# A second level of block products inside one product of an output projection

## The chip, the cores and the metric

The kernel runs on one core of a Trainium2 chip. The metric is the device time of one execution in microseconds (us). A core has five engines that run beside each other, each with its own queue of instructions: TensorE (PE in the profile; it multiplies, and loads its stationary operand as PEld), VectorE (DVE), ScalarE (ACT), GpSimd (POOL) and SyncE (SP), which here only starts transfers. Sixteen DMA engines carry the transfers. Matmul results land in PSUM, which has eight banks of 128 x 512 float32; everything else lies in SBUF or in the chip's main memory.

## The reference

One layer of a trunk with 512 tokens of width 2048, all in float32: a norm, an input projection, windowed attention with sinks, a gate, the output projection, then a gating stage with embeddings and a last norm.

```
hn = rmsnorm(x, norm_g)
q, k, v, gate = split(hn @ w_in)
out = windowed_attention(q, k, v, rel_bias, sinks)     # 512 x 2048
x = x + (out * silu(gate)) @ w_out                     # the output projection
emb = p @ ple_proj
g = sigmoid(rmsnorm(x, ple_norm) @ ple_gate)           # the gating stage
return rmsnorm(x + emb * g, final_g)
```

The change lies in the output projection, a product of a 512 x 2048 matrix (G, the gated attention) with the 2048 x 2048 matrix `w_out`.

## The kernel before, in words

**Precision.** TensorE takes its operands in a shorter format (`fp32r`). So each float32 operand is split into a high part and a low part, and `mm3` (lines 122 to 128) issues three matmuls for one: high x high (L126), high x low (L127), low x high (L128). For weights the high part is a cast on ScalarE (L679, tile `bhi`) and the low part a subtraction on VectorE (L680, tile `blo`). For the left operand it is L784 and L785 (tiles `fho` and `flo`).

**Seven products.** G is cut into four blocks, A11 and A12 (the first 256 tokens, low and high half of the features), A21 and A22 (the other tokens); `w_out` into B11, B12, B21, B22. The four blocks of G x `w_out` (c11 to c22) are built from seven block products instead of eight, each of 256 tokens x 1024 features x 1024 columns. They run in `ORDER_OUT`, 1, 7, 2, 6, 5, 3, 4. Product 2 is A12 x B21 and goes into c11 alone; product 1 (with a minus sign) goes into c11 too. Products 6, 5 and 3 go on adding into the PSUM banks of product 1 (the chain), so between them the banks are read out into x.

**Units and pieces.** A product is done by two calls of `unit`, one for each half `jj` of its columns. A unit takes four pieces of weights (m = 0 to 3). A piece is 128 x 1024: two blocks of 128 features with 512 columns. For a piece TensorE does 2 x 2 x 3 matmuls (two feature blocks, two blocks of 128 tokens, three of `mm3`). After the matmuls of a piece come, in the order in which the program is written: a share of `later` (additions of finished banks into x by `add_y`, L959 or L961, and the squares of finished rows, `squares`, L928, on ScalarE) and `todo` (one step of the next product's left operand, a load of x, or a turn).

**Weights.** `Pieces` hands out the pieces. `get(i)` issues the loads of later pieces and the splits of piece i + 2. There are three buffers each for raw weights, high and low parts; so the split of piece i + 2 waits until TensorE has read piece i - 1. Some products need sums of blocks of weights. These sums (`SUMS`) are made in main memory during attention, each by a copy (SP) and an adding transfer (POOL), in `sum_weights`. The pieces of products 6 and 4 share tiles (`grown`): those of 6 (seeds) are loaded by SP up to six pieces ahead, and once they are split an adding transfer from POOL turns them into those of 4.

**Turns.** In product 4, finished 128 x 128 blocks of x are transposed for the gating stage: `turn` does four transposes on TensorE (L942) and two scaled copies on ScalarE (L945). Product 4 makes 12 turns, two after a piece.

**Order on the engines.** TensorE and SP run in written order throughout (`manual_schedule`). VectorE, ScalarE and POOL have a written order in attention and in the gating stage from its second product on; in the output projection a planner orders them by its own forecast of what is ready. A queue runs in its order whichever way that was made.

Of the kernel before, what the change touches and what calls it, by code (L numbers as in the profile page):

```python
# [55 lines left out]
def trunk_kernel(ctx: ExitStack, tc: tile.TileContext, a: dict):  # L56
# [556 lines left out]

    def blk(t):
        return slice(t * P, (t + 1) * P)

    rooms = []

    ORDER_OUT, ORDER_PLE = (1, 7, 2, 6, 5, 3, 4), (2, 7, 1, 6, 5, 3, 4)

# [5 lines left out]
        return a[nm][2 * (c - 1) + jj, 4 * (r - 1) + m]  # L628

    SUMS = [("w_out", 7), ("w_out", 5), ("w_out", 6), ("ple_gate", 7), ("ple_gate", 5)]  # L630
    for nm, p in SUMS:
        for jj in range(2):
            for m in range(4):
                t = summed[nm, p, jj, m] = tc.dram_tile([P, WE], F32, name=f"{nm}_{p}_{jj}_{m}")
                first = {7: (1, 2), 5: (1, 1)}.get(p)
                copies.append((t, block(nm, *first, jj, m) if first else summed[nm, 7, jj, m]))
                adds.append((t, block(nm, *{7: (2, 2), 5: (1, 2), 6: (1, 1)}[p], jj, m)))
# [9 lines left out]
    class Pieces:  # L647
# [9 lines left out]
        def _prepare(self, i):  # L657
            kind, src, key = self.specs[i]
            if kind == "grow":
                t = self.grown[key]  # L660
                nc.gpsimd.dma_start(t, src, accum_op=ALU.add)
            else:
                if kind == "seed":
                    t = self.grown[key] = rooms[0].tile([P, WE], F32, tag="grown", name=f"grown{i}", bufs=8)
                else:

                    self.raws += 1
                    if rooms and i >= at_ple[ORDER_PLE[0], 0] and self.raws % 4 == 0:
# [24 lines left out]
        def ahead(self, i):  # L693

            last = len(self.specs) - 9
            for n in range(max(i, 0), min(i + 6, last) + 1):
                kind = self.specs[n][0]
                if n not in self.base and n >= self.done and kind != "grow" and (kind == "seed" or n <= i + (4 if i >= at_ple[ORDER_PLE[0], 0] else 3)):
                    self._prepare(n)
            while self.done <= min(i + 2, last):  # L700
                self._split(self.done)
                self.done += 1

        def get(self, i):
            self.ahead(i)

            key = self.specs[i][2]
            if key is not None:
                n = next((n for n in range(i + 1, len(self.specs)) if self.specs[n][2] == key), None)
                if n is not None:  # L710
                    self.due.append((i + 6, n))
            while self.due and self.due[0][0] <= i:
                self._prepare(self.due.pop(0)[1])
            return self.made.pop(i)
# [3 lines left out]
    def add_stage(nm, order):  # L718
        at = {}

        def add_embeds(p, jj):
            if nm == "ple_gate" and p in (1, 5, 3, 4):
                j = jj + 2 * (p in (5, 3))
                B.add("proj", a["ple_proj"].rearrange("(k p) d -> p k d", p=P)[:, :, j * 512 : (j + 1) * 512])

        for p in order:
            for jj in range(2):
                if nm == "ple_gate" and (p, jj) == (4, 0):
                    for v in range(2):
                        at["e", v] = len(B.specs)  # L730
                        add_embeds(p, v)
                at[p, jj] = len(B.specs)
                for m in range(4):
                    if (nm, p) in SUMS:
# [5 lines left out]
                    B.add(kind, src, (nm, jj, m) if p in growing else None)  # L740
                if p != 4:
                    add_embeds(p, jj)
        return at

    at_out = add_stage("w_out", ORDER_OUT)
    at_ple = add_stage("ple_gate", ORDER_PLE)

    class Forms:

# [5 lines left out]
        def steps(self, p):  # L755

            self.made[p] = []
            for h in range(2):
                a11, a21 = self.q[h][:, :, :256], self.q[h][:, :, 256:]
                a12, a22 = self.q[2 + h][:, :, :256], self.q[2 + h][:, :, 256:]  # L760
                if self.nm == "o":
                    src, sub = {
                        1: (a11, None), 7: (a11, (a21, a11)), 2: (a12, None), 6: (a11, (a22, a11)),
                        5: (a21, (a21, a22)), 3: (a12, (a12, a11)), 4: (a22, None),
                    }[p]
                else:
                    src, sub = {
                        2: (a12, None), 7: (a21, (a21, a11)), 1: (a11, None), 6: (a21, (a22, a21)),
                        5: (a11, (a11, a21)), 3: (a12, (a12, a21)), 4: (a22, None),
                    }[p]  # L770
# [129 lines left out]
        for _ in range(-(-len(later) // parts)):  # L900
            later.pop(0)()

    def unit(p, jj, at, forms, todo):

        ps = banks(p, jj, forms.nm)
        f = forms.made[p]
        first = p not in (6, 5, 3)
        for m in range(4):
            bh, bl = B.get(at[p, jj] + m)
            for kk in range(2):  # L910
                k = 2 * m + kk
                fh, fl = f[m]
                for tb in range(2):
                    mm3(ps[tb], fh[:, kk, blk(tb)], fl[:, kk, blk(tb)], bh[kk], bl[kk], first and k == 0, k == 7, not first)
            some_later(4 - m)
            todo()
        return ps


# [27 lines left out]
    ple_forms = Forms(hT, "g")  # L947
    ple_first = ple_forms.steps(2)

    def add_y(p, jj, tb, ps):  # L950
        c11, c12, c21, c22 = ((2 * v + jj, 2 * u + tb) for u in range(2) for v in range(2))
        whither = {
            1: [(c11, -1)], 2: [(c11, 1)], 7: [(c22, 1), (c21, -1)], 6: [(c21, -1)], 5: [(c22, 1)], 3: [(c12, 1)],
            4: [(c21, 1)],
        }[p]
        for (j, t), sign in whither:
            xt = x1[j][:, t, :]
            if sign > 0:
                nc.vector.tensor_add(xt, ps, xt)  # L959
            else:  # L960
                nc.vector.tensor_sub(xt, xt, ps)  # L961
            if p in (2, 5, 3, 4):
                squares(t, j)
# [5 lines left out]
    held = {}  # L969
    for n, p in enumerate(ORDER_OUT):  # L970
        nxt = out_forms.steps(ORDER_OUT[n + 1]) if n < 6 else iter(())
        for jj in range(2):
            later.extend(held.pop(waiting.get((p, jj)), ()))
            calls = iter(range(4))

            def todo():
                part = x_at.get((p, jj, next(calls)))
# [10 lines left out]
            ps = unit(p, jj, at_out, out_forms, todo)  # L988
# [12 lines left out]

# [83 lines left out]

    spare = late.tile([P, 2 * WE], F32R, name="spare")
# [12 lines left out]
    for n, p in enumerate(ORDER_PLE[:-1]):  # L1101
# [8 lines left out]
        for jj in range(2):  # L1110
# [16 lines left out]
            ps = unit(p, jj, at_ple, ple_forms, todo)  # L1127
            e = {}
            if p in (1, 5, 3):
                w = B.get(at_ple[p, jj] + 4)  # L1130
# [14 lines left out]
    def block(jj, tb, tag, e_tag, c=slice(0, 512)):  # L1145

        ps = bank(f"last{jj}_{tb}_{c.start}", tag)
        for k in range(8):
            fh, fl = f[k // 2]
            bh, bl = B.made[at_ple[4, jj] + k // 2]  # L1150
# [155 lines left out]
```

## Time and profile before

| | |
|---|---|
| median of 3 runs | 797.4 us (797.1 to 798.22) |
| the profiled execution | 797.26 us |
| its span, first to last instruction | 795.3 us |
| granted clock of TensorE, mean | 0.996 |
| output projection: matmuls into `o`, 672 | from 451.8 us to 609.3 us |

The profile's page gives for each engine its busy time and its share of the span; a table of groups (line, engine, operation, output <- inputs, shape, count | busy us, mean ns of one | idle time just before them and who ended it); the list of waits (who waited, for whom, in total, times, longest); the transfers; and, for any stretch, the instructions in order of time (start us, duration us, engine, line, operation). A line of stretches reads: from:to, length, then for each engine busy us and number of instructions, the granted clock, the DMA engines' busy share and GB/s. TensorE's matmuls overlap, so the duration of one is longer than the pitch at which they start.

### The profile page before, as it was taken

The page shows a single profiled execution, that of the slowest core. Times are in us where ns is not written, and L with a number is a line of the kernel's source. Part 1 is how long each engine was busy: PE and PEld are TensorE (multiplying, and loading weights), DVE is VectorE, ACT ScalarE, POOL GpSimd, SP SyncE. Part 2 cuts the span into 40 slices and gives each one's busy share as a digit, 9 for nine tenths or more (in the row PEclk, how much of TensorE's full clock was granted, in tenths as well). Part 3 has the DMA queues.
Part 4 walks back from the last instruction along what each step waited for, and adds up shares of the span by engine and source line. Part 5 has one row for each costly group of instructions (what it writes and reads, how often), then busy time and mean ns, then how long its engine had stood idle before and what let it go on. Part 6 is the DMA issues. An engine that isn't in the chain of part 4 may idle for free.

```text
span 795.3 us, 10980 instructions
## 1 busy us (share of the span) xinstructions
PE 785.0 (99%) x3758; PEld 657.6 (83%) x3758; DVE 587.3 (74%) x1026; ACT 500.6 (63%) x1057; POOL 116.2 (15%) x238
## 2 busy tenths in 40 slices
PE   9999999999999999999999999999999999999995
PEld 8888888888888888888888888888888888888885
DVE  4547697877878597777768898766646757988896
ACT  6643576666767576666757655555568656656765
POOL 0021213131212213121212100030000020200000
PEclk9999999999999999999999999999999999999998
DMA  9983489697869968787875479997603996787633
GB/s 348 271 218 110 117 259 242 172 254 183 226 168 255 206 198 230 192 238 158 247 170 146 119 264 328 352 261 239 205 30 132 373 211 194 159 227 218 180 106 106
DMA packets 42919, 165.28 MB, mean 208 GB/s; under 512 B 6048, under 2 KB 7072, under 8 KB 39024
## 3 DMA queue, kind: packets, MB, share of 16 engines
q1 hardware_dynamic: 35456, 129.67, 48.5%
q0 software_dynamic: 7408, 34.93, 23.9%
q8 instruction: 29, 0.48, 0.2%
q14 instruction: 26, 0.21, 0.1%
HBM read 157.70 MB, written 46.19 MB: 256 GB/s over the span
## 4 chain that ended last, share of the span: by engine, by line
PE 98%; DMA 0%; DVE 0%; ACT 0%; issue 0%; ACTq 0%; DVEq 0%
PE gps L126 7%; PE gps L128 7%; PE gps L127 7%; PE qps L126 7%; PE qps L128 7%; PE qps L127 7%; PE o L126 6%; PE o L128 6%; PE o L127 6%; PE g L126 5%; PE g L127 5%; PE g L128 5%; PE s L462 2%; PE o L557 2%; PE vps L279 2%; PE pt L515 2%
## 5 line engine op out<-in xcount | busy, mean ns | idle before, releaser
L680 DVE TENSOR_TENSOR blo<-braw,bhi 128x1024 fp32r<-128x1024 f32 x80 | 97.8, 1222 | 39.7 <-ACT bhi L679 39.5
L679 ACT CAST bhi<-braw 128x1024 fp32r<-128x1024 f32 x80 | 84.2, 1052 | 65.6 <-PE o L128 19.8
L126 PE MATMUL gps<-xh,whi 128*128 128x512 f32 x256 | 99.9, 390 | 0.1
L128 PE MATMUL gps<-xh,wlo 128*128 128x512 f32 x256 | 99.9, 390 | 0.0
L127 PE MATMUL gps<-xl,whi 128*128 128x512 f32 x256 | 99.8, 390 | 0.0
L126 PE MATMUL o<-bhi,fho 128*128 128x512 f32 x224 | 87.7, 392 | 0.0
L126 PE MATMUL qps<-xh,whi 128*128 128x512 f32 x224 | 87.7, 391 | 0.0
L128 PE MATMUL qps<-xh,wlo 128*128 128x512 f32 x224 | 87.4, 390 | 0.0
L127 PE MATMUL qps<-xl,whi 128*128 128x512 f32 x224 | 87.3, 390 | 0.0
L128 PE MATMUL o<-bhi,flo 128*128 128x512 f32 x224 | 87.2, 389 | 0.0
L127 PE MATMUL o<-blo,fho 128*128 128x512 f32 x224 | 87.2, 389 | 0.0
L110 DVE TENSOR_TENSOR wlo<-wraw,whi 128x1024 fp32r<-128x1024 f32 x60 | 73.8, 1231 | 2.7 <-ACT whi L109 2.4
L126 PE MATMUL g<-bhi,fhg 128*128 128x512 f32 x192 | 75.1, 391 | 0.0
L128 PE MATMUL g<-bhi,flg 128*128 128x512 f32 x192 | 74.8, 389 | 0.0
L127 PE MATMUL g<-blo,fhg 128*128 128x512 f32 x192 | 74.7, 389 | 0.0
L531 POOL TENSOR_SCALAR_AFFINE_SELECT own<-r 64x512 fp32r<-64x512 f32 (+1 forms) x48 | 32.5, 677 | 255.8 <-DVE r L521 255.8
L520 ACT CAST r<-pt 128x256 fp32r<-128x256 f32 x64 | 23.8, 371 | 71.5 <-PE pt L515 71.1
L521 DVE TENSOR_TENSOR r<-pt,r 128x256 fp32r<-128x256 f32 x64 | 27.1, 424 | 55.5 <-ACT r L520 54.8
L109 ACT CAST whi<-wraw 128x1024 fp32r<-128x1024 f32 x60 | 62.4, 1041 | 5.3 <-issue 3.9
L680 DVE TENSOR_TENSOR blo<-grown,bhi 128x1024 fp32r<-128x1024 f32 x32 | 39.1, 1224 | 23.5 <-ACT bhi L679 23.4
L128 PEld LDWEIGHTS gps<-xh,wlo 128*128 128x128 f32 x256 | 48.0, 188 | 10.1
L126 PEld LDWEIGHTS gps<-xh,whi 128*128 128x128 f32 x256 | 48.1, 188 | 9.4 <-PE vps L279 0.5
(207 smaller groups left out, 1736.5 us busy)
## 6 DMA issues: line engine op xcount, KB each, us to landing
wraw<-in_w_gate_in SPq DMA_DIRECT2D x32, 512.0 KB, 5.7
wraw<-in_w_q SPq DMA_DIRECT2D x28, 512.0 KB, 5.0
w_out<-in_w_out POOLq DMA_DIRECT2D x24, 512.0 KB, 7.1
braw<-in_w_out SPq DMA_DIRECT2D x24, 512.0 KB, 4.0
braw<-in_ple_gate SPq DMA_DIRECT2D x24, 512.0 KB, 4.2
xw<-in_first SPq DMA_DIRECT2D x14, 640.5 KB, 6.5
w_out<-in_w_out SPq DMA_DIRECT2D x16, 512.0 KB, 5.8
ple_gate<-in_ple_gate SPq DMA_DIRECT2D x16, 512.0 KB, 6.6
```

The source lines that it names most:

```text
L109: nc.scalar.copy(hi, raw)
L110: nc.vector.tensor_sub(lo, raw, hi.bitcast(F32))
L126: nc.tensor.matmul(ps, sh, mh, start=first, stop=False, skip_group_check=more)
L127: nc.tensor.matmul(ps, sh, ml, start=False, stop=False, skip_group_check=more)
L128: nc.tensor.matmul(ps, sl, mh, start=False, stop=last, skip_group_check=more)
L279: nc.tensor.matmul(v_ps[t], h[:, c], both[:, :, 256:512], start=f, stop=e, skip_group_check=True)
L462: nc.tensor.matmul(s_ps[:, u, : 2 * n], st, key[:, :, first : first + n], start=True, stop=True)
L520: nc.scalar.copy(rh, src)
L521: nc.vector.tensor_sub(rl, src, rh.bitcast(F32))
L531: nc.gpsimd.affine_select(out=flat(own), in_=flat(r).bitcast(F32), pattern=[[0, 8], [sign, HB]], compare_op=ALU.is_ge, fill=0.0, base=-HB ...
L679: nc.scalar.copy(hi, raw)
L680: nc.vector.tensor_sub(lo, raw, hi.bitcast(F32))
```

## The change

Product 2 leaves `ORDER_OUT`. In its place A12 x B21 is cut once more, into blocks of 128 tokens x 512 features x 512 columns, and made of seven small products (`small`) of two pieces each. The small products are put between the pieces of products 5, 3 and 4 by the table `SMALL`: 1 and 7 in product 5, 6 and 2 in product 3, 5, 4 and 3 in product 4. A small piece feeds 6 matmuls. The small products 1, 6, 5 and 3 chain in one bank of tag `t`; 4 takes the other bank of `t`, 7 and 2 banks of `o`. Four of the small products use sums of blocks of B21, made with the others during attention (8 more tiles, so 8 copies and 8 adding transfers more). The small left operands are made by `small_form` at the steps listed in `small_steps`. The additions into x go by `add_to_x`, which counts what a block of x still lacks and issues its square after the last.

Beside this: the left operand of product 3 is written over A11 instead of A12 (which the small products still read); a fourth buffer for raw weights is in use from product 6 on instead of from the gating stage on; the adding transfers of product 4's pieces are issued four `get`s later instead of six; the load of `final_g` moves from after product 6 to after product 3; the turns of product 4 come in another order and only through banks of tag `o`, two after each of the four pieces of its first half and after the last two of its second half. From product 7 to the end of product 3, VectorE and ScalarE run in written order.

```
-    ORDER_OUT, ORDER_PLE = (1, 7, 2, 6, 5, 3, 4), (2, 7, 1, 6, 5, 3, 4)
+    ORDER_OUT, ORDER_PLE = (1, 7, 6, 5, 3, 4), (2, 7, 1, 6, 5, 3, 4)
+
+    SMALL = {
+        (5, 0): {1: 1, 3: 1}, (5, 1): {1: 7, 3: 7}, (3, 0): {1: 6, 3: 6}, (3, 1): {1: 2, 3: 2},
+        (4, 0): {0: 5, 1: 5, 2: 4, 3: 4}, (4, 1): {0: 3, 1: 3},
+    }
...
-    for nm, p in SUMS:
+    def small_block(r, c, m):
+
+        return block("w_out", 2, 1, c - 1, 2 * (r - 1) + m)
+
+    for (nm, p), small in zip(SUMS, (7, 5, 6, 4, None)):
+        for m in range(2 if small else 0):
+            t = summed["small", small, m] = tc.dram_tile([P, WE], F32, name=f"small_{small}_{m}")
+            copies.append((t, {
+                7: small_block(1, 2, m), 5: small_block(1, 1, m), 6: summed.get(("small", 7, m)),
+                4: summed.get(("small", 6, m)),
+            }[small]))
+            adds.append((t, small_block(*{7: (2, 2), 5: (1, 2), 6: (1, 1), 4: (2, 1)}[small], m)))
...
-                    if rooms and i >= at_ple[ORDER_PLE[0], 0] and self.raws % 4 == 0:
+                    if rooms and i >= fourth_from and self.raws % 4 == 0:
...
-                    self.due.append((i + 6, n))
+                    self.due.append((i + (6 if i >= at_ple[ORDER_PLE[0], 0][0] else 4), n))
...
+    fourth_from = at_out[6, 0][0]
...
-                        5: (a21, (a21, a22)), 3: (a12, (a12, a11)), 4: (a22, None),
+                        5: (a21, (a21, a22)), 3: (a11, (a12, a11)), 4: (a22, None),
...
             some_later(4 - m)
             todo()
+            between(m)
...
+    def add_to_x(j, t, sign, ps):
+        xt = x1[j][:, t, :]
+        if sign > 0:
+            nc.vector.tensor_add(xt, ps, xt)
+        else:
+            nc.vector.tensor_sub(xt, xt, ps)
+        missing[j, t] -= 1
+        if not missing[j, t]:
+            squares(t, j)
...
+    def small_form(q):
...
+        if sub:
+            nc.vector.tensor_sub(src, *sub)
+            yield
+        if q == 1:
+            nc.scalar.mul(fh, src, -1.0)
...
+        else:
+            nc.scalar.copy(fh, src)
+            nc.vector.tensor_sub(fl, src, fh.bitcast(F32))
+        yield
...
+    small_steps = {
+        (6, 1, 2): 1, (5, 0, 0): 7, (5, 0, 2): 7, (5, 1, 0): 6, (5, 1, 2): 6, (3, 0, 2): 2, (3, 1, 0): 5, (3, 1, 2): 5,
+        (3, 1, 3): 4, (4, 0, 1): 3, (4, 0, 3): 3,
+    }
...
+    def small(q):
+
+        chained = q in (1, 6, 5, 3)
+        n = small_done[q] = small_done.get(q, -1) + 1
+        if n == 0:
+            if q == 1 or not chained:
+                small_ps[q] = bank(f"small{q}", "t" if chained or q == 4 else "o")
+            if chained:
+                small_ps[q] = small_ps[1]
+        bh, bl = B.get(at_out["small", q][n])
+        fh, fl = small_forms[q]
+        for kk in range(2):
+            k = 2 * n + kk
+            mm3(small_ps[q], fh[:, k], fl[:, k], bh[kk], bl[kk], k == 0 and q not in (6, 5, 3), k == 3, q in (6, 5, 3))
+        if n == 1:
+
+            to = {
+                1: [(0, 0, -1)], 2: [(0, 0, 1)], 7: [(1, 1, 1), (0, 1, -1)], 6: [(0, 1, -1)], 5: [(1, 1, 1)],
+                3: [(1, 0, 1)], 4: [(0, 1, 1)],
+            }[q]
+            later[:0] = [partial_of(add_to_x, *v, small_ps[q]) for v in to]
...
-    waiting = {(7, 0): (1, 0), (2, 0): (1, 1)}
+    waiting = {(7, 0): (1, 0), (6, 0): (1, 1)}
...
+        if n == 1:
+
+            middle.enter_context(
+                tc.manual_schedule(engines={getattr(mybir.EngineType, v) for v in ("PE", "SP", "DVE", "Activation")})
+            )
+        if p == 4:
+            middle.close()
...
+            def between(m):
+                q = small_steps.get((p, jj, m))
+                if q is not None:
+                    next(small_made.setdefault(q, small_form(q)))
+                q = SMALL.get((p, jj), {}).get(m)
+                if q is not None:
+                    small(q)
...
-                    for tag in "to":
-                        if turns:
-                            turn(*turns.pop(0), tag)
+
+                    for _ in range({0: 2, 1: 2, 2: 2, 3: 2, 6: 2, 7: 2}.get(4 * jj + step, 0)):
+                        turn(*turns.pop(0), "o")
...
-        if p == 6:
+        if p == 3:
             nc.sync.dma_start(fg, a["final_g"].partition_broadcast(P))
         if p == 3:
-            turns = [(kp, 0) for kp in range(8)] + [(kp, 1) for kp in range(4, 8)]
+            turns = [(kp, th) for kp0, th in ((4, 1), (4, 0), (0, 0)) for kp in range(kp0, kp0 + 4)]
```

More of the change, by code (lines that the diff above doesn't have):

```diff
@@ L697, in ahead @@
                 kind = self.specs[n][0]
-                if n not in self.base and n >= self.done and kind != "grow" and (kind == "seed" or n <= i + (4 if i >= at_ple[ORDER_PLE[0], 0] else 3)):
+                if n not in self.base and n >= self.done and kind != "grow" and (kind == "seed" or n <= i + (4 if i >= fourth_from else 3)):
                     self._prepare(n)
@@ L731, in add_stage @@
                         add_embeds(p, v)
-                at[p, jj] = len(B.specs)
+                at[p, jj] = []
                 for m in range(4):
+                    at[p, jj].append(len(B.specs))
                     if (nm, p) in SUMS:
@@ L740, in add_stage @@
                     B.add(kind, src, (nm, jj, m) if p in growing else None)
+                    q = SMALL.get((p, jj), {}).get(m) if nm == "w_out" else None
+                    if q is not None:
+                        v = at.setdefault(("small", q), [])
+                        src = summed.get(("small", q, len(v)))
+                        if src is None:
+                            src = small_block(*{1: (1, 1), 2: (2, 1), 3: (2, 2)}[q], len(v))
+                        v.append(len(B.specs))
+                        B.add("one", src)
                 if p != 4:
@@ L758, in steps @@
             for h in range(2):
-                a11, a21 = self.q[h][:, :, :256], self.q[h][:, :, 256:]
-                a12, a22 = self.q[2 + h][:, :, :256], self.q[2 + h][:, :, 256:]
+                a11, a21, a12, a22 = (
+                    self.q[v][:, :, c : c + 256] if v in self.q else None for v in (h, 2 + h) for c in (0, 256)
+                )
                 if self.nm == "o":
@@ L901, in some_later, with unit @@
             later.pop(0)()
-    def unit(p, jj, at, forms, todo):
+    def unit(p, jj, at, forms, todo, between=lambda m: None):
         ps = banks(p, jj, forms.nm)
@@ L908, in unit @@
         for m in range(4):
-            bh, bl = B.get(at[p, jj] + m)
+            bh, bl = B.get(at[p, jj][m])
             for kk in range(2):
@@ L948, in trunk_kernel @@
     ple_first = ple_forms.steps(2)
+    missing = {(j, t): {(0, 0): 1, (1, 0): 3, (0, 1): 1, (1, 1): 2}[t // 2, j // 2] for j in range(4) for t in range(NB)}
+    for part, n in {(0, 0): 2, (1, 0): 1, (0, 1): 3, (1, 1): 2}.items():
+        missing[part] += n
+    def add_to_x(j, t, sign, ps):
[7 more added lines that the diff above has]
+            squares(t, j)
@@ new lines, in trunk_kernel @@
+    halves = [gates[2 + h][:, :, :256].rearrange("p k (r t) -> p r k t", r=2) for h in range(2)]
+    sums_at = late.tile([P, 2 * WE], F32, tag="spare", name="small_sums")
+    sigma, tau = (sums_at[:, n * 512 : (n + 1) * 512].rearrange("p (k t) -> p k t", k=4) for n in range(2))
+    small_rooms, small_forms = [], {}
+    def small_form(q):
+        a11, a12, a21, a22 = halves[0][:, 0], halves[1][:, 0], halves[0][:, 1], halves[1][:, 1]
+        src, sub = {
+            1: (a11, None), 2: (a12, None), 4: (a22, None), 7: (sigma, (a21, a11)), 6: (sigma, (a22, sigma)),
+            3: (sigma, (a12, sigma)), 5: (tau, (a21, a22)),
+        }[q]
+        n = len(small_forms)
+        if n % 2 == 0:
+            small_rooms.append(late.tile([P, 2, 2, 512], F32, tag="partial", name=f"small_forms{n}", bufs=2))
+        fh, fl = (
+            small_rooms[-1][:, n % 2, v].bitcast(F32R).rearrange("p (k t) -> p k t", k=4) for v in range(2)
+        )
+        small_forms[q] = fh, fl
+        if sub:
[3 more added lines that the diff above has]
+            nc.scalar.mul(fh, src, -1.0)
+            nc.vector.scalar_tensor_tensor(
+                out=fl, in0=src, scalar=-1.0, in1=fh.bitcast(F32), op0=ALU.mult, op1=ALU.subtract
+            )
+        else:
+            nc.scalar.copy(fh, src)
+            nc.vector.tensor_sub(fl, src, fh.bitcast(F32))
+        yield
@@ new lines, in trunk_kernel @@
+    small_steps = {
+        (6, 1, 2): 1, (5, 0, 0): 7, (5, 0, 2): 7, (5, 1, 0): 6, (5, 1, 2): 6, (3, 0, 2): 2, (3, 1, 0): 5, (3, 1, 2): 5,
+        (3, 1, 3): 4, (4, 0, 1): 3, (4, 0, 3): 3,
+    }
+    small_made = {}
+    small_ps, small_done = {}, {}
+    def small(q):
[15 more added lines that the diff above has]
+                3: [(1, 0, 1)], 4: [(0, 1, 1)],
+            }[q]
+            later[:0] = [partial_of(add_to_x, *v, small_ps[q]) for v in to]
@@ L952, in add_y @@
         whither = {
-            1: [(c11, -1)], 2: [(c11, 1)], 7: [(c22, 1), (c21, -1)], 6: [(c21, -1)], 5: [(c22, 1)], 3: [(c12, 1)],
+            1: [(c11, -1)], 7: [(c22, 1), (c21, -1)], 6: [(c21, -1)], 5: [(c22, 1)], 3: [(c12, 1)],
             4: [(c21, 1)],
@@ L956, in add_y @@
         for (j, t), sign in whither:
[L957 to L963, printed above, removed]
+            add_to_x(j, t, sign, ps)
     turns = []
     x_at = {(1, 1, 1): 0, (7, 0, 0): 2, (7, 0, 3): 1, (7, 1, 1): 3}
-    waiting = {(7, 0): (1, 0), (2, 0): (1, 1)}
+    waiting = {(7, 0): (1, 0), (6, 0): (1, 1)}
     held = {}
+    middle = ExitStack()
     for n, p in enumerate(ORDER_OUT):
-        nxt = out_forms.steps(ORDER_OUT[n + 1]) if n < 6 else iter(())
+        if n == 1:
+            middle.enter_context(
+                tc.manual_schedule(engines={getattr(mybir.EngineType, v) for v in ("PE", "SP", "DVE", "Activation")})
+            )
+        if p == 4:
+            middle.close()
+        nxt = out_forms.steps(ORDER_OUT[n + 1]) if n < 5 else iter(())
         for jj in range(2):
@@ L974, in trunk_kernel @@
             calls = iter(range(4))
+            def between(m):
[3 more added lines that the diff above has]
+                q = SMALL.get((p, jj), {}).get(m)
+                if q is not None:
+                    small(q)
             def todo():
-                part = x_at.get((p, jj, next(calls)))
+                step = next(calls)
+                part = x_at.get((p, jj, step))
                 if part is not None:
@@ L981, in todo @@
                 if p == 4:
-                    for tag in "to":
-                        if turns:
-                            turn(*turns.pop(0), tag)
+                    for _ in range({0: 2, 1: 2, 2: 2, 3: 2, 6: 2, 7: 2}.get(4 * jj + step, 0)):
+                        turn(*turns.pop(0), "o")
                     if jj:
                         next(ple_first, None)
-            ps = unit(p, jj, at_out, out_forms, todo)
+            ps = unit(p, jj, at_out, out_forms, todo, between)
             posts = [partial_of(add_y, p, jj, tb, ps[tb]) for tb in range(2)]
@@ L1084, in trunk_kernel @@
     moved = []
-    spare = late.tile([P, 2 * WE], F32R, name="spare")
+    spare = late.tile([P, 2 * WE], F32R, tag="spare", name="spare")
     rooms4 = {}
@@ L1129, in trunk_kernel @@
             if p in (1, 5, 3):
-                w = B.get(at_ple[p, jj] + 4)
+                w = B.get(at_ple[p, jj][3] + 1)
                 for t in (0, 1) if p in (1, 3) else (2, 3):
@@ L1149, in block @@
             fh, fl = f[k // 2]
-            bh, bl = B.made[at_ple[4, jj] + k // 2]
+            bh, bl = B.made[at_ple[4, jj][k // 2]]
             mm3(ps[:, c], fh[:, k % 2, blk(tb)], fl[:, k % 2, blk(tb)], bh[k % 2][:, c], bl[k % 2][:, c], k == 0, k == 7)
```

## The prediction

> **What bounds the kernel now.** I read the profile's page first, then the list of waits, then single stretches. The page's first two parts and the waits of TensorE:
>
> ```profile
> span 795.3 us, 10980 instructions
> PE 785.0 (99%) x3758; PEld 657.6 (83%) x3758; DVE 587.3 (74%) x1026; ACT 500.6 (63%) x1057; POOL 116.2 (15%) x238
> L126 PE MATMUL o<-bhi,fho 128*128 128x512 f32 x224 | 87.7, 392 | 0.0
> ...
> PE warm_ps L141 <- PEq L1296: 0.9, 1, 0.9
> PE qps L265 <- ACT xh L224: 0.2, 1, 0.2
> ```
>
> TensorE is busy for 99% of the span, and its list of waits has two rows in all, both before the first real matmuls, 1.1 us together. From there to the last few microseconds it waits for nobody. So a matmul taken out of the middle is worth its pitch, and any wait put there costs its full length: nothing absorbs it. The pitch is not the 392 ns of the row, because matmuls overlap; it is the number started in a full stretch. The same stretches show how full the other engines and the DMA are (first the matmuls into `o` alone, then all):
>
> ```profile
> core 0: us, PE busy (x), PEclk, DMA share, GB/s
> 452.00:582.00 130.00, 130.00 (x575) 1.00 0.79 259
> ...
> core 0: us, PE busy (x) PEld busy (x) DVE busy (x) ACT busy (x) POOL busy (x), PEclk, DMA share, GB/s
> 100.00:450.00 350.00, 350.00 (x1730) 294.56 (x1730) 271.47 (x594) 235.23 (x645) 78.02 (x168) 1.00 0.78 205
> 452.00:496.00 44.00, 44.00 (x195) 36.43 (x195) 40.07 (x49) 23.97 (x31) 0.00 (x0) 1.00 0.78 274
> 496.00:541.00 45.00, 45.00 (x200) 37.26 (x200) 32.83 (x38) 24.41 (x33) 6.89 (x8) 1.00 0.98 293
> 541.00:582.00 41.00, 41.00 (x183) 33.96 (x182) 25.27 (x26) 21.58 (x31) 0.00 (x0) 1.00 0.61 206
> 582.00:610.00 28.00, 28.00 (x149) 23.71 (x148) 15.62 (x19) 22.41 (x45) 0.00 (x0) 1.00 0.11 38
> ```
>
> 575 matmuls in 130.00 us is 226 ns each. A piece of weights feeds 12 of them, 2.71 us; a product (8 pieces) takes 21.7 us.
>
> **Part 1: fewer matmuls.** Product 2 is 96 matmuls. The seven small ones are 7 x 2 pieces x 6 = 84. So 12 x 226 ns = **-2.71 us**. The 128x128 stationary and the 512 columns stay, so the pitch stays. Number and grouping of the transposes stay (12 turns in six pairs). [...]
>
> **Part 2: more side work.** Product 2's 8 pieces become 14, so six more splits; 4 more additions to x (8 instead of 4); form copies 7 instead of 4, and four small subtractions. Durations from the groups and the order of time before:
>
> ```profile
> L680 DVE TENSOR_TENSOR blo<-braw,bhi 128x1024 fp32r<-128x1024 f32 x40 | 48.9, 1223 | 20.0 <-ACT bhi L679 19.9
> L679 ACT CAST bhi<-braw 128x1024 fp32r<-128x1024 f32 x40 | 42.0, 1051 | 31.8 <-PE o L128 19.8 <-DMA braw<-w_out 7.6 <-DVE blo L680 2.1
> L785 DVE TENSOR_TENSOR flo<-gate,fho 128x512 fp32r<-128x512 f32 x24 | 16.5, 687 | 5.7 <-ACT fho L784 5.7
> L784 ACT CAST fho<-gate 128x512 fp32r<-128x512 f32 x23 | 14.3, 624 | 19.9 <-PE o L127 19.8
> L959 DVE TENSOR_TENSOR x1s<-o,x1s 128x512 f32<-128x512 f32 x20 | 13.1, 684 | 1.5 <-PE o L128 1.5
> ...
> 549.66 1.28 DVE L959 TENSOR_TENSOR x1s<-o,x1s 128x512 f32<-128x512 f32 x2
> 550.00 1.05 ACT L679 CAST bhi<-braw 128x1024 fp32r<-128x1024 f32 x1 [1.52 <-PE o L128]
> 550.96 0.62 ACT L928 ACTIVATE junk<-x1s 128x512 f32<-128x512 f32 x1
> 551.09 1.23 DVE L680 TENSOR_TENSOR blo<-braw,bhi 128x1024 fp32r<-128x1024 f32 x1
> 551.58 0.61 ACT L928 ACTIVATE junk<-x1s 128x512 f32<-128x512 f32 x1
> 552.46 0.62 ACT L784 CAST fho<-gate 128x512 fp32r<-128x512 f32 x1 [0.17 <-PE o L127]
> 552.99 1.04 ACT L679 CAST bhi<-braw 128x1024 fp32r<-128x1024 f32 x1
> ```
>
> VectorE gets 6 x 1.22 + 4 x 0.68 + 3 x 0.69 + 4 x 0.68 = 14.8 us more, on the 113.8 us that the four stretches from 452 to 610 add up to; ScalarE 6 x 1.05 + 3 x 0.62 = 8.2 us on 92.4. In some 155 us both still fit, at 83% and 65%. By total work this costs nothing. What can cost is order.
>
> **Part 3: less cover per piece, and a written order.** A piece is split two pieces ahead: its high part (ScalarE, L679) may start when TensorE leaves the buffer three pieces back, then VectorE makes the low part. With pieces of 2.71 us that is 5.42 us of cover. A small piece is 6 matmuls, 1.36 us; wherever one lies in the pair, cover is 4.07 us. The chain itself takes 0.2 us (release) + 1.08 (high, to the start of low) + 1.22 = 2.5 us, so 2.9 us of margin become 1.55.
>
> In the stretch before, the planner orders VectorE and ScalarE by what is ready. The change writes their order for products 7, 6, 5 and 3: split, addition to x, its square, forms, next split. What a written order costs is seen in the gating stage, which has one already:
>
> ```profile
> 677.90 0.68 DVE L1025 TENSOR_TENSOR s<-e,s 128x512 f32<-128x512 f32 x1
> 678.62 0.69 DVE L1029 TENSOR_TENSOR x1s<-x1s,s 128x512 f32<-128x512 f32 x1
> 679.34 0.63 ACT L1032 ACTIVATE s<-x1s 128x512 f32<-128x512 f32 x1 [1.29 <-DVE x1s L1029]
> 680.55 1.22 DVE L680 TENSOR_TENSOR blo<-grown,bhi 128x1024 fp32r<-128x1024 f32 x1
> 680.67 0.63 ACT L1032 ACTIVATE s<-x1s 128x512 f32<-128x512 f32 x1 [0.60 <-DVE x1s L1029]
> 681.30 2.20 ACT L679 CAST bhi<-grown 128x1024 fp32r<-128x1024 f32 x2
> 682.20 0.39 PE L126 MATMUL g<-bhi,fhg 128*128 128x512 f32 x1
> ```
>
> ScalarE stands 1.29 and 0.60 us at the squares until VectorE has added, and the split behind them starts late. The low part begun at 680.55 ends at 681.77, and its piece begins at 682.20: of 2.9 us of margin 0.4 are left. With 1.55 us such a meeting is a stall. [...]
>
> One place worked out, the last three pieces of product 5 and the first of product 3, from the start of (5, second half, m=1) as zero. TensorE starts: m=1 at 0, small 7 at 2.71, m=2 at 4.07, m=3 at 6.78, small 7 again at 9.49, product 3 at 10.85, its low part one matmul later, 11.1. ScalarE's written order: high of m=2 at 0.2; VectorE its low at 1.3, then the addition at 2.4 (1.14 us after the low's start), done at 3.1; square at 3.15; form copy 3.8; high of m=3 4.3, high of the small piece 5.3. VectorE: lows at 5.4 and 6.5, second addition 7.7, done 8.35. Square 8.4, the small form's copy 9.0, and only then the high of product 3's first piece, 9.55, though its buffer has been free since 7.0; low 10.65 to 11.87. Needed at 11.1: 0.8 us late, and 1.0 with the 0.2 that VectorE carries in. Stepping all of 7, 6, 5 and 3 through the written order in this way gives stalls at four places: 0.4 us where (6, second half) waits for the last addition of product 1, 1.0 us here, 1.5 us at (3, second half, m=0 and 1), 1.4 us at (3, second half, m=2) and the first piece of product 4. Together **+4.3 us**. Ends: 0, if the meetings fall as well as in the planner's order, where TensorE has no wait; 5.9, if ScalarE needs 0.88 us after each square (551.58 to 552.46) instead of 0.62.
>
> **Part 4: product 4.** Here the planner orders again, but six small pieces and all turns in the two `o` banks meet. ScalarE has 24 hT copies as before, and 14 pieces where there were 8. Ends: 0, as in the planner's product 4 before (no wait of TensorE), and 6.5 us, which stepping it in written order would give. The nearest row is the planner's own, so I take **+0.5 us**.
>
> **Part 5: transfers.** Four sums of two pieces add 8 copies and 8 accumulations to 40 and 40 while attention runs; six more loads; a fourth buffer two stages earlier; final_g moves from after product 6 to after product 3.
>
> ```profile
> braw<-w_out SPq DMA_DIRECT2D x16, 512.0 KB, 5.0
> x1s<-in_x SPq DMA_DIRECT2D x4, 1024.0 KB, 6.8
> grown<-w_out SPq DMA_DIRECT2D x8, 512.0 KB, 8.5
> grown<-in_w_out POOLq DMA_DIRECT2D x8, 512.0 KB, 10.5
> fg<-in_final_g SPq DMA_DIRECT2D x1, 1024.0 KB, 17.4
> ```
>
> Attention's DMA share of 0.78 rises by at most a fifth, to 0.94; the copies and accumulations are queued behind nothing that TensorE wants soon, since an attention weight is loaded two pieces, over 10 us, ahead. On POOL's queue eight more issues lie between masks. The seeds of product 6 now load beside x, in a stretch at 0.78, and the growing transfers follow at once beside the first pieces of product 5; a seed is asked for up to six pieces (16 us) ahead and lands in 8.5 us, a plain piece three or four ahead and in 5.0. final_g leaves the full stretch (0.98) for the empty one (0.11); TensorE waited for it nowhere, so that gains nothing. I take 0 for all of it; bounds -0.2 and +2 us, the latter being a wait of ScalarE for `braw<-w_out` that reaches TensorE where its group above has 7.6 us of them hidden.
>
> **Sum.** The profiled execution took 797.26 us (span 795.3 and 1.96 around it). 797.26 - 2.71 + 4.3 + 0.5 = **799.3 us**. The median of 797.4 is 0.14 above that execution, well inside what can be told apart: 0.2%, 1.6 us.
>
> **Rivals.**
> 1. *The queues keep up* (the other side). No handover is late; TensorE's list of waits stays empty and only part 1 remains: 797.26 - 2.71 = 794.6. It decides wherever the addition and its square are done within the 1.55 us of margin. For it: by total work both engines have room. Against: the 0.4 us left in the gating stage with longer pieces.
> 2. *Product 4 clogs.* The planner lines ScalarE up for readiness, and the four copies of two turns stand ahead of highs whose cover is now one small and one full piece; half to all of 6.5 us: 799.3 + 3 to 6 = 802 to 805. For it: ScalarE is busy 22.41 of 28 us there already.
> 3. *Part of the price:* only one or two of the four places stall, 1.1 to 4 us together, and the change is not measurable: 796 to 798.9.
>
> **How the numbers follow.** Forecast (798 to 801.5) 0.46, of which 0.06 lies under 799.0; rival 1 0.28; rival 2 0.12; rival 3 0.14. Faster than 795.8: 0.28. Between 795.8 and 799.0: 0.14 + 0.06 = 0.20. Slower: 0.40 + 0.12 = 0.52. The likeliest one's own range is 798 to 801.5; 8 in 10 need rival 1's end and the lower half of rival 2: 794.4 to 803.
>
> **What would show it.** Right: matmuls into `o` and the small banks 660 instead of 672; in TensorE's list of waits rows of some 1 us each, released by VectorE's low parts (L680's line), at about 547, 563 and 577 us; ScalarE waiting for VectorE at the squares there. Part 4 right: no such rows, or short ones, in product 4. Part 5 wrong: releases by transfers. The prediction is wrong if TensorE's busy time falls by 2.7 us and its idle time doesn't grow.

## The result and the profile after

The changed kernel takes 800.89 us (median of 6 runs, 800.65 to 802.06) against 797.49 us before (6 runs). The ratio is 1.0045, with a 95% interval of 1.0032 to 1.0058: it is slower by 3.4 us. The forecast was 799.3 us, slower. Of all the executions reported below one is far off, 2055.76 us in experiment 5, and it is not in the ratio there.

The profiled execution of the changed kernel is a long one of the six, 802.06 us. Its page and TensorE's list of waits (engine, line, waited for: us in total, times, longest):

```profile
span 800.4 us, 11030 instructions
PE 785.9 (98%) x3746; PEld 655.2 (82%) x3746; DVE 599.9 (75%) x1043; ACT 506.7 (63%) x1066; POOL 123.5 (15%) x246
...
PE o L127 <- DVE blo L699: 4.7, 5, 1.6
PE warm_ps L141 <- PEq L1415: 0.9, 1, 0.9
```

The 12 matmuls are gone (3746 instructions instead of 3758), and a row has come that was not there: TensorE waits for low parts of weights (L699 is the old L680). The row's 4.7 us count only from the modelled end of the matmul before, so they understate what is lost. The number of matmuls that start in a stretch tells it better:

```profile
core 0: us, PE busy (x) PEld busy (x) DVE busy (x) ACT busy (x) POOL busy (x), PEclk, DMA share, GB/s
496.00:541.00 45.00, 44.42 (x194) 36.00 (x193) 38.42 (x46) 23.27 (x29) 6.92 (x8) 1.00 0.97 280
541.00:582.00 41.00, 36.88 (x155) 28.21 (x154) 33.16 (x39) 25.80 (x40) 0.00 (x0) 1.00 0.63 212
582.00:615.00 33.00, 33.00 (x172) 27.85 (x171) 23.66 (x26) 26.84 (x50) 0.00 (x0) 1.00 0.34 112
100.00:450.00 350.00, 350.00 (x1731) 294.54 (x1730) 271.26 (x596) 235.64 (x645) 84.46 (x176) 1.00 0.85 229
```

From 541 to 582 us 155 matmuls start where 183 did before: 28 x 226 ns = 6.3 us. From 496 to 541 six fewer start, 1.4 us. From 582 us on, in product 4, TensorE is full again, and attention has as many matmuls as before (1731 and 1730) although its DMA share went from 0.78 to 0.85. So the loss sits in products 6, 5 and 3 and at the first piece of 4. The 7.7 us lost and the 2.7 us saved leave 5.0 us; the two profiled executions stand 4.8 us apart. That is more than the 3.4 us between the medians, since the profiled execution of the changed kernel lies 1.2 us above its median: by the medians the stalls cost 3.4 + 2.7 = 6.1 us.

The place that the prediction worked out, in the order of time (start us, duration us, engine, line, operation; in brackets the idle time before, and who ended it):

```profile
543.00 1.22 DVE L699 TENSOR_TENSOR blo<-braw,bhi 128x1024 fp32r<-128x1024 f32 x1
544.13 0.68 DVE L989 TENSOR_TENSOR x1s<-o,x1s 128x512 f32<-128x512 f32 x1
544.85 0.63 ACT L959 ACTIVATE junk<-x1s 128x512 f32<-128x512 f32 x1 [2.08 <-DVE x1s L989]
545.48 0.60 ACT L1024 CAST small_forms<-small_sums 128x512 fp32r<-128x512 f32 x1
545.79 0.39 PE L126 MATMUL small<-bhi,small_forms 128*128 128x512 f32 x1
545.99 2.94 ACT L698 CAST bhi<-braw 128x1024 fp32r<-128x1024 f32 x3
547.15 0.44 PE L126 MATMUL o<-bhi,fho 128*128 128x512 f32 x1
547.46 2.35 DVE L699 TENSOR_TENSOR blo<-braw,bhi 128x1024 fp32r<-128x1024 f32 x2
548.73 0.50 PE L127 MATMUL o<-blo,fho 128*128 128x512 f32 x1 [1.14 <-DVE blo L699]
549.06 0.39 PE L128 MATMUL o<-bhi,flo 128*128 128x512 f32 x1
```

ScalarE stands idle for 2.08 us at the square of a row until VectorE has added to it. Then it copies a small form, and only at 545.99 does it begin the high part of product 3's first piece. VectorE's low part follows at 547.46 and is done at 548.68. TensorE had begun that piece at 547.15 with the high part; its second matmul comes at 548.73, 1.58 us after the first where 0.23 us is usual. The third comes 0.33 us later, not 0.23: this stall costs another 0.1 us after it.

### The profile page after: what moved, and what is told of

Read it like the earlier page. It is cut to its first block, busy times and chain, and to the rows that moved or that the text cites. A ratio compares the mean times of both kernels' runs of the same rounds, so it can differ in the third digit from the quotient of the medians.

```text
span 800.4 us, 11030 instructions
## 1 busy us (share of the span) xinstructions
PE 785.9 (98%) x3746; PEld 655.2 (82%) x3746; DVE 599.9 (75%) x1043; ACT 506.7 (63%) x1066; POOL 123.5 (15%) x246
## 4 chain that ended last, share of the span: by engine, by line
PE 95%; DVE 2%; DMA 1%; ACT 1%; issue 1%; ACTq 0%; DVEq 0%
PE gps L126 7%; PE gps L128 7%; PE gps L127 7%; PE qps L126 7%; PE qps L128 7%; PE qps L127 7%; PE g L126 5%; PE g L127 5%; PE g L128 5%; PE o L127 5%; PE o L128 5%; PE o L126 5%; PE s L462 2%; PE o L557 2%; PE vps L279 2%; PE pt L515 2%
## 5 line engine op out<-in xcount | busy, mean ns | idle before, releaser
L699 DVE TENSOR_TENSOR blo<-braw,bhi 128x1024 fp32r<-128x1024 f32 x86 | 104.6, 1222 | 45.9 <-ACT bhi L698 45.7
L698 ACT CAST bhi<-braw 128x1024 fp32r<-128x1024 f32 x86 | 89.9, 1052 | 70.9 <-PE g L128 19.1
L127 PE MATMUL o<-blo,fho 128*128 128x512 f32 x192 | 75.6, 394 | 4.7 <-DVE blo L699 4.7
L126 PE MATMUL o<-bhi,fho 128*128 128x512 f32 x192 | 75.4, 393 | 0.0
L128 PE MATMUL o<-bhi,flo 128*128 128x512 f32 x192 | 74.8, 390 | 0.0
L495 ACT ACTIVATE t<-t,sm 128x129 f32<-128x129 f32 x128 | 50.6, 397 | 8.0 <-DVE sm L491 6.4
```

What stands on the lines that cost most here:

```text
L126: nc.tensor.matmul(ps, sh, mh, start=first, stop=False, skip_group_check=more)
L127: nc.tensor.matmul(ps, sh, ml, start=False, stop=False, skip_group_check=more)
L128: nc.tensor.matmul(ps, sl, mh, start=False, stop=last, skip_group_check=more)
L495: nc.scalar.activation(su, su, AF.Exp, bias=sm[:, u : u + 1], accum_out=sm[:, 2 + u : 3 + u])
L698: nc.scalar.copy(hi, raw)
L699: nc.vector.tensor_sub(lo, raw, hi.bitcast(F32))
```

## The experiments

The theory: in written order, ScalarE's queue holds the square of a finished row in front of the next split; the square waits for VectorE, and with the shorter cover of a small piece the split is then late. Rival A: the shorter cover is late under any order. Rival B: transfers land late, since more of them share the time. Each experiment ran with the kernel before on the same chip; ratios are to that.

**1. The planner's order again.** In the change, the block that writes the order is taken out:

```
-            middle.enter_context(
-                tc.manual_schedule(engines={getattr(mybir.EngineType, v) for v in ("PE", "SP", "DVE", "Activation")})
-            )
+            pass
```

> The change, but VectorE and ScalarE are ordered by the planner again in products 7, 6, 5 and 3. Theory (the written order puts a square, which waits for VectorE, in front of the next split): the waits of TensorE for low parts go, 794.8 us (797.5 - 2.7) to 795.6. Rival A (the shorter cover of small pieces is late under any order): about 800.9, as the change. Rival B (transfers land late): 800 to 801, with waits of the splits for loads as before them.

Measured: 796.48 us, ratio 0.9988 (0.9979 to 0.9997). Rival A falls: the same small pieces with the same cover, in another order, are 4.4 us faster. But the theory's range is missed by 0.9 us, and only 0.9 of the 2.7 us that the matmuls save are seen. TensorE's waits, in an execution of 797.39 us:

```profile
PE o L127 <- DVE blo L699: 2.3, 2, 1.5
PE warm_ps L141 <- PEq L1413: 0.9, 1, 0.9
PE o L126 <- ACT bhi L698: 0.3, 1, 0.3
```

Two stalls stay, at about 494 and 533 us. Before both, ScalarE is idle until a load lands, 0.66 and 2.70 us. At the first, VectorE then takes three steps for left operands (from 491.52 to 493.4) before the low part, which starts 2.1 us after the high part:

```profile
491.24 1.06 ACT L698 CAST bhi<-braw 128x1024 fp32r<-128x1024 f32 x1 [0.66 <-DMA braw<-w_out]
493.32 1.21 DVE L699 TENSOR_TENSOR blo<-braw,bhi 128x1024 fp32r<-128x1024 f32 x1
...
531.93 2.06 ACT L698 CAST bhi<-braw 128x1024 fp32r<-128x1024 f32 x2 [2.70 <-DMA braw<-w_out]
533.01 1.22 DVE L699 TENSOR_TENSOR blo<-braw,bhi 128x1024 fp32r<-128x1024 f32 x1 [2.53 <-ACT bhi L698]
```

**2. The written order without the small pieces.** The kernel before, with the same block around products 7 to 3:

```
+        if n == 1:
+            middle.enter_context(
+                tc.manual_schedule(engines={getattr(mybir.EngineType, v) for v in ("PE", "SP", "DVE", "Activation")})
+            )
+        if p == 4:
+            middle.close()
```

> The kernel before, with VectorE and ScalarE in written order from product 7 to product 3 and nothing else changed. Theory (written order costs only together with small pieces): margins of 2.9 us shrink but stay above zero, 797.3 to 798.0. If the written order cost the same with any pieces it would be 797.5 + 4 to 6 = 801.5 to 803.5. Rival A expects no change, 797.5.

Measured: 798.41 us, ratio 1.0009 (1.0000 to 1.0018): 1.0 us between the medians, nothing to 1.4 us by the interval; the median lies 0.4 us above the theory's range. The two waits that count, of ScalarE from 496 to 582 us and of TensorE in the whole span (of an execution of 797.69 us, one of the shortest of the eleven):

```profile
ACT junk L928 <- DVE x1s L959: 21.0, 10, 2.8
...
PE o L127 <- DVE blo L680: 0.4, 1, 0.4
```

ScalarE stands at its squares even longer here (21.0 us, ten times) than in the changed kernel (14.4 us, six times, in the same stretch), and yet a single short wait reaches TensorE. So neither the order alone nor the small pieces alone cost the 3.4 us: the two together do. The reading is that the order uses up margin, and that the small pieces have taken most of it away; that it is their shorter cover, and not what else came with them (more additions, forms and loads), is worked out in the prediction and not tested by itself.

**3. The square behind the next split.** In the change, still in written order, a finished row's square is put on a list, and the list is emptied right after the next `get` of a unit:

```
     def squares(t, j):
+        owed.append((t, j))
+
+    def square(t, j):
...
             bh, bl = B.get(at[p, jj][m])
+            owed_squares()
```

> The change, still in written order; only each square of a finished row is issued behind the next piece's split instead of in front of it. Theory: ScalarE no longer stands at a square while a split is due; stepping the queues gives 0.4 us of stall instead of 4.3, so 795.2, and up to 796.2 if the late load at about 530 us still costs its 0.7. Rival A: 800.9. Rival B: 800 to 801.

Measured: 795.30 us, ratio 0.9972 (0.9961 to 0.9983). It beats both kernels. No low part appears in TensorE's list of waits (by the starts of its matmuls two short stalls stay, 0.4 us each at 507 and 531 us), and around the same place as above ScalarE splits when TensorE releases the buffer and does the square afterwards:

```profile
PE warm_ps L141 <- PEq L1425: 0.8, 1, 0.8
PE o L126 <- DVE x1s L1001: 0.2, 1, 0.2
...
537.50 1.06 ACT L698 CAST bhi<-braw 128x1024 fp32r<-128x1024 f32 x1 [1.11 <-PE o L128]
538.14 0.68 DVE L999 TENSOR_TENSOR x1s<-o,x1s 128x512 f32<-128x512 f32 x1
538.86 1.06 ACT L698 CAST bhi<-braw 128x1024 fp32r<-128x1024 f32 x1 [0.30 <-PE small L128]
539.81 0.63 ACT L969 ACTIVATE junk<-x1s 128x512 f32<-128x512 f32 x1
540.44 0.61 ACT L1034 CAST small_forms<-small_sums 128x512 fp32r<-128x512 f32 x1
541.62 1.06 ACT L698 CAST bhi<-braw 128x1024 fp32r<-128x1024 f32 x1 [0.57 <-ACT small_forms L1034]
```

The addition that a square needs is done by 538.8, a split before ScalarE comes to it at 539.81: the same work, moved behind one instruction, waits for nobody.

**4. Plain loads into the growing pieces.**

```
-                nc.gpsimd.dma_start(t, src, accum_op=ALU.add)
+                nc.gpsimd.dma_start(t, src)
```

> The change, with the transfers from POOL into the growing pieces as plain loads instead of accumulating ones (the sums of weights of the last product of both stages are left out, so its result is another). Rival B: the 8 accumulating transfers crowd out the loads, so most of the stall goes, 796 to 797. Theory: only the stall where a split waited for a load (about 532 us, 0.7 us) goes, 799.8 to 800.4. Rival A: 800.9.

Measured: 799.98 us, ratio 1.0031 (1.0020 to 1.0043), 0.9 us less than the change between the medians; the two intervals overlap. Transfers from 490 to 535 us, first in the change, then here (tile, queue, count, size, median us to landing; and of POOL's queue, q0, packets, MB, share of the 16 engines' time):

```profile
braw<-w_out SPq DMA_DIRECT2D x8, 512.0 KB, 8.8
grown<-in_w_out POOLq DMA_DIRECT2D x8, 512.0 KB, 14.5
q0 software_dynamic: 1152, 4.19, 46.8%
```

```profile
braw<-w_out SPq DMA_DIRECT2D x8, 512.0 KB, 4.2
grown<-in_w_out POOLq DMA_DIRECT2D x8, 512.0 KB, 6.6
q0 software_dynamic: 1152, 4.19, 24.2%
```

The same bytes landed in less than half the time when they didn't accumulate (6.6 us instead of 14.5), and the eight loads beside them too (4.2 instead of 8.8). The stalls at about 532 and 543 us go. Those after 546 us stay, and the list of waits still has 3.5 us for low parts. So rival B is right about a part, and only that. The stall at 543 us is not the loads' alone: it goes in experiment 3 too, where the transfers accumulate as before. In the change ScalarE had stood at a square before that piece's split:

```profile
539.64 0.63 ACT L959 ACTIVATE junk<-x1s 128x512 f32<-128x512 f32 x1 [2.99 <-DVE x1s L989]
540.78 1.05 ACT L698 CAST bhi<-braw 128x1024 fp32r<-128x1024 f32 x1
```

After the late load at 531 us VectorE came late to the addition that this square needs: it begins it 3.2 us ahead of the piece's first matmul (538.92 and 542.15), and 4.2 us ahead with plain loads (536.62 and 540.78). The square passed that on.

**5. The cure on the kernel before.** Experiment 2 with the edit of experiment 3.

> The kernel before with VectorE and ScalarE in written order from product 7 to product 3, and each square behind the next piece's split. Theory: the one stall that the written order gave the kernel before goes with the square, 797.2 to 797.8. If that stall had another cause it stays, 798.0 to 798.5.

Measured: 797.31 us, ratio 0.9994 (0.9986 to 1.0003). Against experiment 2 the medians stand 1.1 us apart and the intervals barely touch: the cost of the written order is gone, as far as they tell; ScalarE's wait at the squares is 0.2 us instead of 21.0.

**6. Cure and plain loads together.** Experiments 3 and 4 in one.

> The change with the squares behind the next split and with plain loads in place of the 8 + 16 accumulating transfers into the growing pieces (so the sums of the last product of both stages are left out). Theory: what is left of the stalls, 0.3 us at a late load and 0.3 us at the last addition of product 1, shrinks to the second: 794.7 to 795.1. If transfers cost more than the late load shows, 793.5 to 794.5.

Measured: 794.82 us, ratio 0.9967 (0.9956 to 0.9979). TensorE's list of waits has only the start left. It is 2.8 us below the kernel before, which is what 12 matmuls are worth (1.7 to 3.5 us by the interval). The medians of this and experiment 3 stand 0.5 us apart, which their intervals don't tell apart, so late loads cost little that shows once the squares are out of the way.

**7. A double dose in the same place.** In the change, each square is followed by a second one into another buffer:

```
         nc.scalar.activation(junk, x1[j][:, t, :], AF.Square, accum_out=ssq2[:, t, j : j + 1])
+        again = late.tile([P, 512], F32, tag="junk", name=f"again{j}_{t}", bufs=3)
+        nc.scalar.activation(again, x1[j][:, t, :], AF.Square)
```

> The change, each square of a finished row done twice, in the same place in front of the next split (16 more on ScalarE, 0.6 us each, 10 us of work). Theory: each of the meetings is later by the second square; stepping the queues gives 3.2 to 3.7 us more stall, so 804.0 to 804.6. Rival A (short cover alone): about 800.9. Rival B (transfers): 800.9.

Measured: 803.83 us, ratio 1.0081 (1.0068 to 1.0094): 2.9 us more than the change, just under the 3.2 to 3.7 that stepping gave. TensorE now also waits for high parts:

```profile
PE o L127 <- DVE blo L699: 4.8, 6, 1.1
PE o L126 <- ACT bhi L698: 1.0, 3, 0.4
```

**8. The same dose behind the split.** Experiment 3 with the second square.

> The change with the squares behind the next split, and each done twice there. Theory: the same 10 us of extra work on ScalarE costs nothing in this place, 795.0 to 795.8. If ScalarE's total work were the bound, 798 to 799.

Measured: 795.18 us, ratio 0.9972 (0.9963 to 0.9982), the same as experiment 3. Sixteen more squares cost ScalarE the same work here as in experiment 7 (514.5 us busy there, 515.4 here), and the time nothing that the medians show. The profiled execution is the longest of the eight, 796.9 us, and in it TensorE waits 1.3 us for low parts, at about 494 and 533 us. Before the first ScalarE stood idle for 3.33 us until a load landed; that stretch has no square yet. So amount of work is not the cause; its place is.

**9. VectorE alone in written order.** In the change's block "Activation" is struck out.

> The change with VectorE alone in written order in products 7, 6, 5 and 3; ScalarE is ordered by the planner. Theory (it is the square on ScalarE's queue that stands in front of the split): most of the stall goes, 795.5 to 797, as with both planned. If VectorE's order were the cause by itself, 799.5 to 801.

Measured: 795.51 us, ratio 0.9971 (0.9960 to 0.9982). With ScalarE planned, its wait at the squares from 496 to 582 us is 0.2 us, and in TensorE's list one row of 0.2 us for a low part is left. VectorE's written order by itself costs nothing that shows. It is ScalarE's queue.

**10. Product 1's last additions first.** In experiment 3, the additions held back from product 1 go to the front of the list:

```
-            later.extend(held.pop(waiting.get((p, jj)), ()))
+            later[:0] = held.pop(waiting.get((p, jj)), ())
```

> The squares behind the next split, and product 1's last additions in front of product 7's in the list of later work. Theory: the short stall at the second half of product 6 (0.3 us at 507 us) goes, 794.8 to 795.3; nothing else moves. It is a size that the interval may not tell.

Measured: 794.89 us, ratio 0.9965 (0.9952 to 0.9977). TensorE's row for the addition (0.2 us in experiment 3) is gone from its list, and one of 0.4 us for a low part, at about 532 us, is in it instead; the 0.4 us between the medians is not told apart by the intervals.

## Why the prediction was right, and where a size was off

The direction and the mechanism were right, and so were the four places; the price was too low. The sum had 4.8 us of stalls (4.3 and 0.5); by the medians 6.1 us came. Part of the nearness is luck: the 0.5 us stood for product 4, where nothing waits, and covers a part of what was missing elsewhere.

*Part 1, -2.71 us.* Right: with nearly all stalls gone (experiments 6 and 10) the kernel is 2.8 and 2.9 us below the one before, with intervals of about 0.9 us to either side.

*Part 2, more side work, 0.* Right, and by more than it needed: experiment 8 puts 10 us on top. The work itself was put a little high: VectorE's busy time grew by 12.6 us instead of 14.8 (587.3 to 599.9), ScalarE's by 6.1 instead of 8.2.

*Part 3, +4.3 us.* The mechanism is shown by experiments 1, 2, 3, 7, 8 and 9. The sum is what was mis-sized. Stall by stall in the profiled execution, from the starts of TensorE's matmuls (what exceeds 226 ns, with the matmul after it), against the four places of the forecast:

| place | forecast | changed kernel |
|---|---|---|
| (6, second half), last addition of product 1 | 0.4 | 0.3 |
| (5, second half), m=0 and m=3 | none | 1.7 |
| product 3, first piece | 1.0 | 1.5 |
| (3, second half), m=0 and 1 | 1.5 | 1.6 |
| (3, second half), m=2 (in the run m=3, 0.2), and product 4, first piece | 1.4 | 2.2 |
| sum | 4.3 | 7.3 |

Three things were missing. The pair in product 5 starts with a late load, whose delay the square of experiment 4's last lines passes on; plain loads take both away. In experiment 4's execution, without the pair, the other places add up to 5.5 us. After each wait the next matmul is late by another 0.1 us, about 1 us over the table. And the first piece of product 4 lost about 0.8 us more than forecast. VectorE's order of time there:

```profile
575.85 1.38 DVE L989 TENSOR_TENSOR x1s<-o,x1s 128x512 f32<-128x512 f32 x2 [0.47 <-PE o L128]
577.15 0.68 DVE L1025 TENSOR_TENSOR small_forms<-small_sums,small_forms 128x512 fp32r<-128x512 f32 x1
577.90 0.69 DVE L989 TENSOR_TENSOR x1s<-small,x1s 128x512 f32<-128x512 f32 x1
578.51 1.21 DVE L699 TENSOR_TENSOR blo<-grown,bhi 128x1024 fp32r<-128x1024 f32 x1
```

ScalarE's high part was done at 577.61, but the low part starts at 578.51, behind three additions that the program writes later, in product 4. The planner, free again from there on, had put them between instructions whose order among themselves was fixed. That it did so is seen; what its forecast was is not.

The 0.4 us of margin that Part 3 reads in the gating stage is not the squares' doing. The low part begun at 680.55 had its high part from 678.06 on and stood behind four additions and products on VectorE; and counted to the second matmul, at 682.42, 0.65 us were left. The stepping doesn't use it; what was said against rival 1 does.

*Part 4, +0.5 us for product 4.* Inside product 4 there is no wait: 0. What the planner did cost stands at its first piece, on VectorE and not on ScalarE (the 0.8 us above). Rival 2 didn't come.

*Part 5, transfers, 0.* Mis-sized: 0.9 us by the medians of experiment 4, inside its bounds (-0.2 and +2), and not clear of the intervals. The step that failed is "a plain piece three or four ahead and in 5.0": beside the growing transfers, pieces landed in 8.8 us. The 16 transfers more in attention cost nothing, as forecast (1731 and 1730 matmuls in 350 us).

*The order of the queues.* The forecast needs a split that doesn't pass the square in front of it, and on ScalarE none did. In the changed kernel it stood idle for 2.08 us until the square at 544.85, and the split behind began at 545.99, although the last matmul of the piece in its buffer had ended at 542.31. Over the stretch from 496 to 582 us such waits add up to 14.4 us. The stepping takes VectorE to run in order in the same way; no run shows that by itself.

*Rival 1, "the queues keep up", 794.6.* It gave the other side its right price: 794.8 to 795.3 is what the kernel takes once the squares are out of the way. It fell for the place of one kind of instruction.

What stays open: which part of the 0.5 us between experiment 3 and the full gain is late loads and which is chance between runs; why the load that the split before 494 us needs took 8.5 us in the profiled execution of experiment 1 and 9.7 in that of experiment 8, but 7.2 to 8.1 in those of the change and of experiments 3, 4, 6, 7, 9 and 10; and how much of experiment 1's stall there is that load, and how much the three steps ahead of the low part.

## What to carry to other kernels

When work is saved on the busiest engine by cutting it into smaller steps, the cover of everything prepared ahead shrinks with the steps (here, by the forecast's count, from 5.42 us to 4.07); work out that cover against the longest chain across two queues, and not against their totals. In a written order, put what waits for another queue (here a square that needs an addition) behind what is already due: here no split passed a waiting square, and in the changed kernel ScalarE stood 14.4 us at six of them. Doubling a suspected instruction in its place, and again in the cured place, tells place from amount in two runs.

## What was not expected of the hardware

In the changed kernel TensorE was back at its pitch only one matmul after a wait: wherever a matmul of the table waited and the one behind it didn't, the next start came 0.33 to 0.34 us on (548.73 to 549.06) instead of 0.23. Each of these stalls cost that 0.1 us beyond the wait itself. Why is not shown.

Accumulating transfers slowed others beyond what their bytes say: the eight plain loads of the same stretch landed in 8.8 us beside accumulating ones and in 4.2 us beside plain ones, with 4.19 MB in 1152 packets on POOL's queue in both. Accumulating, these packets took 46.8% of the 16 engines' time from 490 to 535 us, as plain ones 24.2%.
